# Homes of two experts in float32 at a time, and 18 load slots, in a two-layer trunk with a routed feed-forward

## The chip, the cores and the metric

The kernel runs on one core of a Trainium2 chip. The metric is the device time of one execution, in microseconds (us), as the median of three runs.

## The reference, cut to what matters

Two layers act on `x` (256 tokens of 1024 numbers, float32). Each has a mixing part (attention, pooling, memory attention, gates) and a feed-forward part. That of layer 0 is dense; that of layer 1 sends each token to two of eight experts:

```
logits = ht @ w_router
vals, idx = lax.top_k(logits, TOP_K)
gates = jax.nn.softmax(vals, axis=-1)
comb = einsum('tk,tke->te', gates, one_hot(idx, N_EXPERTS))
for e in range(N_EXPERTS):
    out = out + comb[:, e:e + 1] * ((silu(ht @ w1[e]) * (ht @ w3[e])) @ w2[e])
```

Here `ht` is the RMS-normalised `x`, with gain `norm_ffn`. The weights of one expert are three matrices of 1024 x 3584 float32.

## The kernel before, in words

All weights stream through one class, `Stream` (lines 154 to 242), in an order that `plan` (line 48) writes out. A load is 1 MB (128 partitions of 2048 float32) and holds two units. SP issues the loads in that order, and each goes into a slot, which is a tile of the name given to `widen` (line 180). `load` (line 194) issues a load for every slot in the deque `free`; `give` (line 224) puts a slot back after its second unit has been used, and calls `load`. `widen(tags, uses)` limits how often a slot serves, and `retire` (line 186) takes a slot out: at once if it is free, else after the load that it holds.

Up to the end of layer 1's mixing part every weight is split by ACT and DVE into a high and a low float32r part (`split`, line 207) and PE multiplies three combinations (line 391). The experts' weights are used as float32 straight from the slot. The eight places of experts are filled with the routed experts so that place p has `ROWS[p]` rows: 96, 64, 96, 96, 64, 96, 96, 64. "Expert" means such a place below. Layer 1 then goes like this:

- The router: `logits` while the last tall product runs, then the top two, `pos`, `place` (the slot of a token in its expert, lines 979 to 993) and the reciprocal norm `rx[3]`.
- Lines 997 to 999: `x` times `rx[3]` is split into two float32r tiles `xs` in the homes B0 and B1.
- `prep_g` (line 1002) makes G, a 0/1 matrix of tokens by rows, in the home `bb`, for a list of experts. `prep_t` (line 1012) has PE transpose it and ACT copy it into GT (home E5), which holds all experts. `gather` (line 1022) multiplies `xs` by G (line 1040) to bring the rows of the experts into XG, with the gain put on by ACT and DVE in turn (lines 1044, 1046).
- Expert 0 is gathered at once, into E2. Experts 1 to 4 are gathered together (320 columns) into E6 and E7, and 5 to 7 (256 columns) into E2; which, when and where stands in `GROUPS` (line 1222).
- `half_all` (line 1132) computes half of expert 0's first 512 inner columns for all tokens, from `h2T` (homes E6, E7), and `sel_T` picks its rows with `G[0]`.
- `STEPS` is the list of 8 experts x 7 chunks of 512 inner columns. In turn i the loop at line 1223 runs `up(i)` (line 1157: four loads, w1 and w3) and `down(i - 1)` (line 1190: two loads, w2). Both work on 32 x 32 pieces of PE: line 1172 into `acc`, line 1198 into `y`. For each unit `pump` (line 354) takes one piece of side work from the deques `fa` and `fb`.
- After an expert's last chunk `down` copies `y` to `yf` in pieces of 32 x 256, odd j by DVE (line 1212) and even j by ACT (line 1214). A bank of `y` holds two groups of 32 rows (`y[r // 2]`). `evac_split` (line 363; here lines 365, 366) makes a high and a low part, and `scatter` (line 1118) multiplies GT by both and adds the weighted result to `total` (line 1126).
- After the loop `finish` (line 841) writes the result.

The slots, by name: raw0 to raw3 from the start; E0, E1, E3, E2 (one use) and bias from line 900; E4, E5, A1, A0 from line 954, in the middle of the last tall products; pair0 to pair3 from line 1227, after `half_all`, where A1 and E5 are retired because `total` and GT need them. E2 serves once, as XG needs it.

Of the kernel before, what the change touches and what calls it, by code (L numbers as in the profile page):

```python
# [10 lines left out]
F32 = mybir.dt.float32  # L11
# [7 lines left out]
D = 1024  # L19
# [226 lines left out]
def trunk(ctx: ExitStack, tc: tile.TileContext, a, out, stage=99):  # L246
# [651 lines left out]
    parts = mix(1, hold["hT"], rx[2], hold["mT"], rm)  # L898

    W.widen(("E0", "E1", "E3"))  # L900
    W.widen(("E2",), 1)
    W.widen(("bias",))
    misc = own("band", [128, 1088], name="misc")
    used = [0]

# [47 lines left out]

    ss = branch_end(1, *parts, ready_moe, lambda: W.widen(("E4", "E5", "A1", "A0")))
    drain()
    if stage == 2:
        finish((nc.gpsimd, nc.gpsimd))
        return
# [35 lines left out]
    count = ms([128, NE])  # L994
    nc.vector.tensor_copy(count, pos[:, 2])
    rstd_of(rx[3], ss)
    xs = [own(t, [128, 2, D], F32R, name="xs") for t in ("B0", "B1")]
    for tb in range(2):
        evac_split(x[:, tb], xs[0][:, tb], xs[1][:, tb], rx[3][:, tb:tb + 1])
    G, XG, GT = {}, {}, []  # L1000

    def prep_g(es):

        at = np.cumsum([0] + [ROWS[e] for e in es])
        g = own("bb", [128, 2, at[-1]], F32R, name="G")
        for j, e in enumerate(es):
            G[e] = g[:, :, at[j]:at[j + 1]]
            for tb in range(2):
                nc.vector.tensor_scalar(G[e][:, tb], slot[:, :ROWS[e]], place[:, tb, e:e + 1], None, op0=OP.is_equal)
        G[tuple(es)] = g  # L1010

    def prep_t(e):

        if not GT:
            GT.append(own("E5", [max(ROWS), NE, 2, 128], F32R, name="GT"))
        t = mbank("gTp", (128, 2, 128))
        n = ROWS[e]
        for tb in range(2):
            nc.tensor.transpose(t[:n, tb], G[e][:, tb].bitcast(F32), ident)
        nc.scalar.activation(GT[0][:n, e], t[:n], AF.Copy)  # L1020

    def gather(es, homes):


        at = np.cumsum([0] + [ROWS[e] for e in es])
        n = at[-1]
        per = 1 if n > 256 else 2 if n > 128 else 4
        each = 8 // len(homes)

        def part(k0):  # L1030
            if k0 == 0:
                tiles = [own(t, [128, each, n], name="xg") for t in homes]
                for j, e in enumerate(es):
                    XG[e] = lambda k, j=j: tiles[k // each][:, k % each, at[j]:at[j + 1]]
                XG[tuple(es)] = lambda k: tiles[k // each][:, k % each]
            t = mbank("xgp", (128, per, n))
            for i in range(per):
                ps = [(p[:, tb, (k0 + i) * 128:(k0 + i + 1) * 128], G[tuple(es)][:, tb]) for p in xs for tb in range(2)]
                for m, (s, g) in enumerate(ps):
                    nc.tensor.matmul(t[:, i], s, g, start=m == 0, stop=m == len(ps) - 1)  # L1040
            for i in range(per):
                k = k0 + i
                if k % 2:
                    nc.vector.tensor_scalar(XG[tuple(es)](k), t[:, i], col("norm_ffn", 1, k), None, op0=OP.mult)
                else:
                    nc.scalar.activation(XG[tuple(es)](k), t[:, i], AF.Copy, scale=col("norm_ffn", 1, k))

        return [lambda k0=k0: part(k0) for k0 in range(0, 8, per)]

    prep_g([0])  # L1050
    for f in gather([0], ["E2"]):
        f()
    oh = ms([128, 2, 2, NE])
    vm, gates = ms([128, 2, 2]), ms([128, 2, 2])
# [62 lines left out]

    def scatter(e, ys, tb, j):
        t = mbank("sc")
        for p in range(2):  # L1120
            nc.tensor.matmul(t, GT[0][:ROWS[e], e, tb], ys[p][:, j * 512:(j + 1) * 512], start=p == 0, stop=p == 1)  # L1121
        if not total:
            total.append(own("A1", [128, 2, D], name="total"))
        sl = slice(j * 512, (j + 1) * 512)
        xo = total[0][:, tb, sl]
        nc.vector.scalar_tensor_tensor(xo, t, comb[:, tb, e:e + 1], x[:, tb, sl] if e == 0 else xo,  # L1126
                                       op0=OP.mult, op1=OP.add)
# [4 lines left out]
    def half_all():  # L1132


        accs = [acc_tile() for _ in range(2)]
        gs = []

        def ep():
            for tb in range(2):
                g = junk()[:, :256]  # L1140
                nc.scalar.activation(g, accs[tb][0][:, :256], AF.Silu, scale=rx[3][:, tb:tb + 1])
                nc.vector.scalar_tensor_tensor(g, accs[tb][1][:, :256], rx[3][:, tb:tb + 1], g, op0=OP.mult, op1=OP.mult)
                gs.append(g)

        def sel_T():
            t = mbank("ge0", (128, 2, ROWS[0]))
            for q in range(2):
                for tb in range(2):
                    nc.tensor.matmul(t[:, q], gs[tb][:, q * 128:(q + 1) * 128], G[0][:, tb].bitcast(F32),
                                     start=tb == 0, stop=tb == 1)  # L1150
            for q in range(2):
                nc.scalar.activation(gts[0][:, :, q], t[:, q].rearrange("p (r t) -> p r t", r=3), AF.Copy)

        run(pairs_of(256), st_of(h2T), lambda tb, b: accs[tb][b], 2, ep)
        fa.append(sel_T)

    def up(i, e, width):
# [7 lines left out]
        for k0 in range(0, 8, count):  # L1165
            w, home = W.raw()
            for m in range(count):
                k = k0 + m
                for r in range(nr):
                    t, c0 = acc[r // per], r % per * n  # L1170
                    for j in TILES:
                        nc.tensor.matmul(t[32 * j:32 * j + 32, c0:c0 + n], XG[e](k)[:, 32 * r:32 * r + 32],  # L1172
                                         w[:, (4 * m + j) * n:(4 * m + j + 1) * n],
                                         start=k == 0 and r % per == 0, stop=k == 7, tile_position=(0, 32 * j), skip_group_check=True)
            W.give(home)
            if k0 + count < 8:
                pump()
# [12 lines left out]
    def down(i, e, first, last):  # L1190
        gt = gts.pop(i)
        n = ROWS[e]
        for q in range(4):
            w, home = W.raw()
            for r in range(n // 32):
                t, c0 = y[r // 2], r % 2 * 256
                for j in TILES:
                    nc.tensor.matmul(t[32 * j:32 * j + 32, c0:c0 + 256], gt[:, r, q], w[:, 256 * j:256 * j + 256],  # L1198
                                     start=first and q == 0 and r % 2 == 0, stop=last and q == 3,
                                     tile_position=(0, 32 * j), skip_group_check=True)  # L1200
            W.give(home)
            if q < 3:
                pump()
        if last:
            yf = work.tile([n, D], F32, tag="S4", name="yf", bufs=3)
            yh, yl = (work.tile([n, D], F32R, tag="S4", name="ys", bufs=3) for _ in range(2))
            for r in range(n // 32):
                for j in TILES:
                    o = yf[32 * r:32 * r + 32, 256 * j:256 * j + 256]
                    v = y[r // 2][32 * j:32 * j + 32, r % 2 * 256:r % 2 * 256 + 256]  # L1210
                    if j % 2:
                        nc.vector.tensor_copy(o, v)  # L1212
                    else:
                        nc.scalar.activation(o, v, AF.Copy)  # L1214
            evac_split(yf, yh, yl)
            fb.extend([lambda: None] * 2)
            for b in range(2):
                for tb in range(2):
                    fb.append(lambda tb=tb, b=b: scatter(e, (yh, yl), tb, b))
        pump()  # L1220

    GROUPS = {0: ([1, 2, 3, 4], ["E6", "E7"]), 4: ([5, 6, 7], ["E2"])}
    for i in range(len(STEPS) + 1):
        if i == 0:
            new_gt(0)
            half_all()
            W.widen([f"pair{j}" for j in range(PAIRB)])
            W.retire(("A1", "E5"))
            W.load()
            places()  # L1230
            up(0, 0, 64)
        elif i < len(STEPS):
            e, c = STEPS[i]
            if e in GROUPS and c == 3:
                es, homes = GROUPS[e]
                if e == 0:
                    fb.append(lambda: prep_t(0))
                fb.append(lambda es=es: prep_g(es))
                fb.extend([lambda e_=e_: prep_t(e_) for e_ in es])
                fb.extend(gather(es, homes))  # L1240
            new_gt(i)
            up(i, e, 128)
        if i >= 1:
# [1 line left out]
            if i == 1:  # L1245
                drain()
            if c2 == 0:
                y = [pm.tile([128, 512], F32, tag=f"y{b}", name=f"y{b}", bufs=1) for b in range(-(-ROWS[e2] // 64))]
            down(i - 1, e2, c2 == 0, c2 == FE // 512 - 1)
    drain()  # L1250
    where = plan()[1]
# [117 lines left out]
```

## Time and profile before

| | us |
|---|---|
| median of three runs | 1659.22 |
| lowest, highest | 1658.77, 1660.36 |
| the profiled execution | 1658.55 |
| its span, first to last instruction | 1656.8 |
| PE busy in the span | 1615.1 |
| DVE busy | 651.0 |
| ACT busy | 529.7 |

One execution was traced. PE is TensorE's matrix products, PEld its weight loads, DVE is VectorE, ACT ScalarE, SP the engine that issues the loads. Times of the trace count from the start of the span. Each matrix product of float32 operands shows as two PE instructions, one of float32r operands as one. Busy PE is not PE at its peak: ends of products are modelled. The granted clock of PE is given as a share of its full 2.4 GHz; the other level is 1.2 GHz. A line of the chain is start, duration and what was on it; "x24" is a count of instructions, and some per cent of PE's records are missing.

### The profile page before, as it was taken

The numbers are of one execution on the slowest core, as the hardware profiler recorded it, in microseconds if no ns is written. First come the engines' busy times: TensorE is split into PE (matmuls) and PEld (weight loads), VectorE is DVE, ScalarE is ACT, GpSimd is POOL, SyncE is SP. The second block draws the span as 40 slices with busy tenths as digits, with TensorE's granted clock in tenths as the row PEclk, the third lists the DMA queues.
The fourth block names the chain that finished last, engine by engine and source line by source line (L and its number), as shares of the span: only waits on it lengthen the run. The fifth ranks groups of instructions, "written<-read, shape, count | busy, mean of one in ns | idle before, by whom it ended". The sixth has DMA issues, their size and how long they took to land.

```text
span 1656.8 us, 40623 instructions
## 1 busy us (share of the span) xinstructions
PE 1615.1 (97%) x18103; PEld 1119.8 (68%) x18103; DVE 651.0 (39%) x1270; ACT 529.7 (32%) x898; POOL 8.4 (1%) x37
## 2 busy tenths in 40 slices
PE   9999999999999999999999999999999999999986
PEld 6887778788888887788756555665655556556543
DVE  6676876555555767776310202002011020110201
ACT  6675755544554666645210100001010010100100
POOL 0000000000000000000000000000000000000000
PEclk9999999999999999999999999999999999999998
DMA  9534455444554434666779999999999999999994
GB/s 376 202 148 155 148 206 184 178 178 178 181 194 172 174 137 165 232 231 235 300 285 390 414 418 418 417 417 419 418 418 413 418 418 417 417 418 407 416 414 195
DMA packets 69606, 493.86 MB, mean 298 GB/s; under 512 B 7888, under 2 KB 7888, under 8 KB 10544
## 3 DMA queue, kind: packets, MB, share of 16 engines
q1 hardware_dynamic: 67680, 485.55, 74.1%
q0 software_dynamic: 1312, 5.08, 1.0%
q8 instruction: 144, 2.36, 0.6%
q10 hardware_dynamic: 432, 0.56, 0.1%
q14 instruction: 38, 0.31, 0.1%
HBM read 490.11 MB, written 1.05 MB: 296 GB/s over the span
## 4 chain that ended last, share of the span: by engine, by line
PE 83%; DMA 13%; DVE 2%; ACT 1%; issue 0%; SPq 0%; ACTq 0%; DVEq 0%; POOLq 0%
PE acc L391 41%; PE acc L1172 22%; DMA raw<-in_w_dram 13%; PE y L1198 12%; PE sc L1121 1%; PE ds L641 1%; DVE yf L1212 1%; PE xgp L1040 1%; PE tT L503 1%; PE do L677 1%; PE dt L666 1%; ACT yf L1214 0%; ACT ys L365 0%; PE mo L586 0%; PE ms L553 0%
## 5 line engine op out<-in xcount | busy, mean ns | idle before, releaser
L1172 PE MATMUL acc<-raw,xg 128*32 128x256 f32 (+1 forms) x9408 | 533.6, 378 | 11.4 <-DMA raw<-in_w_dram 10.8
L1172 PEld LDWEIGHTS acc<-raw,xg 128*32 128x32 f32 x9408 | 305.2, 110 | 220.5 <-issue 18.8
L219 DVE TENSOR_TENSOR pair<-raw,pair 128x1024 fp32r<-128x1024 f32 (+1 forms) x247 | 300.4, 1219 | 212.3 <-ACT pair L218 211.8
L391 PE MATMUL acc<-pair,bigB 128*128 128x512 f32 x1536 | 378.4, 401 | 1.8 <-DVE pair L219 1.7
L218 ACT ACTIVATE pair<-raw 128x1024 fp32r<-128x1024 f32 (+1 forms) x247 | 260.2, 1056 | 304.5 <-PE acc L391 289.5
L391 PEld LDWEIGHTS acc<-pair,bigB 128*128 128x128 f32 x1536 | 284.9, 189 | 67.7 <-DVE pair L219 2.1
L1183 DVE TENSOR_TENSOR junk<-acc,junk 128x256 f32<-128x256 f32 (+2 forms) x90 | 30.4, 369 | 624.0 <-ACT junk L1182 624.0
L1198 PE MATMUL y<-raw,gt 128*32 128x256 f32 x4704 | 269.0, 379 | 6.7 <-DMA raw<-in_w_dram 6.6
L1182 ACT ACTIVATE junk<-acc 128x256 f32<-128x256 f32 (+2 forms) x90 | 30.8, 343 | 681.9 <-PE acc L1172 680.3
L1198 PEld LDWEIGHTS y<-raw,gt 128*32 128x32 f32 x4704 | 153.8, 110 | 110.1 <-issue 7.8
L391 PE MATMUL acc<-pair,bigA 128*128 128x512 f32 (+1 forms) x960 | 219.9, 386 | 0.7 <-ACT g L814 0.3
L391 PEld LDWEIGHTS acc<-pair,bigA 128*128 128x128 f32 x960 | 172.3, 188 | 39.1 <-ACT g L814 0.8
L391 PE MATMUL acc<-pair,E 128*128 128x512 f32 x456 | 109.1, 396 | 0.9 <-DVE E L738 0.9
L391 PEld LDWEIGHTS acc<-pair,E 128*128 128x128 f32 x456 | 84.6, 188 | 20.3 <-DVE E L738 1.8
L1121 PE MATMUL sc<-ys,GT 96*128 96x512 f32 (+1 forms) x64 | 27.6, 506 | 12.4 <-ACT ys L365 12.0
L1185 DVE STREAM_TRANSPOSE gt<-junk 128x128 f32<-128x128 f32 (+1 forms) x147 | 34.5, 282 | 0.8
L1212 DVE COPY yf<-y 32x256 f32<-32x256 f32 x42 | 17.7, 422 | 41.0 <-ACT yf L1214 40.4
L1121 PEld LDWEIGHTS sc<-ys,GT 96*128 96x128 f32 (+1 forms) x64 | 11.4, 211 | 29.7 <-ACT ys L365 15.8
L1126 DVE SCALAR_TENSOR_TENSOR total<-sc,misc,total 128x512 f32<-128x512 f32 x28 | 20.6, 749 | 26.0 <-PE sc L1121 25.9
L1214 ACT ACTIVATE yf<-y 32x256 f32<-32x256 f32 x42 | 15.7, 374 | 47.0 <-PE y L1198 38.6
L646 DVE CUSTOM_DVE_ANT_0 dp<-ds,bias 128x128 f32<-128x128 f32 (+1 forms) x64 | 20.8, 353 | 21.6 <-PE ds L641 21.5
L650 ACT ACTIVATE dp<-dp,dmn 128x128 f32<-128x128 f32 (+1 forms) x64 | 28.5, 446 | 1.8 <-DVE dmn L646 1.2
(243 smaller groups left out, 780.0 us busy)
## 6 DMA issues: line engine op xcount, KB each, us to landing
raw<-in_w_dram SPq DMA_DIRECT2D x455, 1024.0 KB, 20.0
bb<-in_b_gate_dram POOLq DMA_DIRECT2D x6, 512.0 KB, 4.3
E<-in_mem_t_dram SPq DMA_DIRECT2D x2, 1024.0 KB, 11.4
raw<-in_w_dram SPq DMA_DIRECT2D x4, 256.0 KB, 10.5
raw<-in_w_dram SPq DMA_DIRECT2D x2, 512.0 KB, 13.0
x<-in_x_dram SPq DMA_DIRECT2D x1, 1024.0 KB, 14.1
E<-in_mem_dram SPq DMA_DIRECT2D x1, 1024.0 KB, 19.9
bias<-in_bias_dram POOLq DMA_DIRECT2D x1, 1024.0 KB, 7.5
```

The costliest lines, as they stand in the source:

```text
L218: nc.scalar.activation(t[:, 0, sl], src[:, sl], AF.Copy)
L219: nc.vector.tensor_tensor(t[:, 1, sl], src[:, sl], t[:, 0, sl].bitcast(F32), OP.subtract)
L391: nc.tensor.matmul(accs(tb, b)[:, :n], s, w[:, off:off + n], start=begin and (tb, b) not in started, stop=end and n_ == 2 and last[b] == ( ...
L646: nc.vector.tensor_tensor_reduce(p[:, 0, m, :kl], t[m][:, :kl], bias[:, h, 256 - kl:], 1.0, 3e38, OP.add, OP.min, mn[:, m:m + 1])
L650: nc.scalar.activation(p[:, 1, m, :kl], p[:, 0, m, :kl], AF.Exp, scale=-1.0, bias=mn[:, m:m + 1], accum_out=s0[:, b, h:h + 1] if m == 0 el ...
L1121: nc.tensor.matmul(t, GT[0][:ROWS[e], e, tb], ys[p][:, j * 512:(j + 1) * 512], start=p == 0, stop=p == 1)
L1172: nc.tensor.matmul(t[32 * j:32 * j + 32, c0:c0 + n], XG[e](k)[:, 32 * r:32 * r + 32], w[:, (4 * m + j) * n:(4 * m + j + 1) * n], start=k = ...
L1182: nc.scalar.activation(g[:, r0:r1], v[:, :, 0], AF.Silu)
L1183: nc.vector.tensor_tensor(g[:, r0:r1], v[:, :, 1], g[:, r0:r1], OP.mult)
L1185: nc.vector.transpose(gts[i][:, r, 4 - width // 32:].rearrange("p q t -> p (q t)"), g[:, r])
L1198: nc.tensor.matmul(t[32 * j:32 * j + 32, c0:c0 + 256], gt[:, r, q], w[:, 256 * j:256 * j + 256], start=first and q == 0 and r % 2 == 0, st ...
L1212: nc.vector.tensor_copy(o, v)
```

## The change

- `xs` and its split go. G is made with `rx[3]` as its value in place of 1, and the gather multiplies `x` itself by G, both float32, two products for each block in place of four.
- Expert 0's XG and G sit in a tile of the tag S4; a second tile there, `here`, holds a 0/1 matrix for `sel_T`. The others are gathered for two experts at a time, [1, 2], [3, 4], [5, 6], [7], in turns of chunk 3 of experts 0, 2, 4, 6, in E6 and E7 by turns, with G in the same tile.
- GT holds two experts, in `bb`. `prep_t` runs once in each expert, and DVE makes GT as 1 where the transposed G is above 0.
- One bank of the gathered rows is evacuated by ACT, the next by DVE.
- E2 and E5 stay slots, B0 and B1 become slots after the last tall product, E7 serves as a slot twice after `half_all`. Only A1 is retired.
- `y` always has two banks; row group r lies in bank r % 2, and is copied by DVE for odd r, by ACT for even r.
- The last expert's rows are scattered as float32 without the split.

```diff
-    W.widen(("E2",), 1)
-    W.widen(("bias",))
+    W.widen(("E2", "bias"))
...
     drain()
+    W.widen(("B0", "B1"))
...
-    xs = [own(t, [128, 2, D], F32R, name="xs") for t in ("B0", "B1")]
-    for tb in range(2):
-        evac_split(x[:, tb], xs[0][:, tb], xs[1][:, tb], rx[3][:, tb:tb + 1])
-    G, XG, GT = {}, {}, []
+    G, XG, GT, flags = {}, {}, {}, {}
+    back = own("bb", [max(ROWS), 2, 2, 128], F32R, name="GT")
...
+        n = at[-1]
+        home = tile_([128, 10 * n])
+        XG[tuple(es)] = home[:, :8 * n].rearrange("p (k a) -> p k a", k=8)
+        g = home[:, 8 * n:].rearrange("p (t a) -> p t a", t=2)
...
+                nc.vector.tensor_scalar(G[e][:, tb], slot[:, :ROWS[e]], place[:, tb, e:e + 1], rx[3][:, tb:tb + 1],
+                                        op0=OP.is_equal, op1=OP.mult)
...
-            nc.tensor.transpose(t[:n, tb], G[e][:, tb].bitcast(F32), ident)
-        nc.scalar.activation(GT[0][:n, e], t[:n], AF.Copy)
+            nc.tensor.transpose(t[:n, tb], G[e][:, tb], ident)
+        GT[e] = back[:n, e % 2]
+        nc.vector.tensor_scalar(GT[e], t[:n], 0.0, None, op0=OP.is_gt)
...
+        per = 2 if n > 128 else 4
...
+                for tb in range(2):
+                    nc.tensor.matmul(t[:, i], x[:, tb, (k0 + i) * 128:(k0 + i + 1) * 128], G[tuple(es)][:, tb],
+                                     start=tb == 0, stop=tb == 1)
...
+                if k0 // per % 2:
+                    nc.vector.tensor_scalar(XG[tuple(es)][:, k], t[:, i], col("norm_ffn", 1, k), None, op0=OP.mult)
...
-    prep_g([0])
-    for f in gather([0], ["E2"]):
+    prep_g([0], lambda shape: s4(shape, "xg"))
+    here = s4([128, 2, ROWS[0]], "here")
+    for tb in range(2):
+        nc.vector.tensor_scalar(here[:, tb], slot, place[:, tb, 0:1], None, op0=OP.is_equal)
+    for f in gather([0]):
...
+        gt = GT[e] if len(ys) == 2 else GT[e].bitcast(F32)
+        for p in range(len(ys)):
+            nc.tensor.matmul(t, gt[:, tb], ys[p][:, j * 512:(j + 1) * 512], start=p == 0, stop=p == len(ys) - 1)
...
-                t, c0 = y[r // 2], r % 2 * 256
+                t, c0 = y[r % 2], r // 2 * 256
...
+            for j in TILES:
+                for r in range(n // 32):
                     o = yf[32 * r:32 * r + 32, 256 * j:256 * j + 256]
+                    v = y[r % 2][32 * j:32 * j + 32, r // 2 * 256:r // 2 * 256 + 256]
+                    if r % 2:
                         nc.vector.tensor_copy(o, v)
                     else:
                         nc.scalar.activation(o, v, AF.Copy)
+            ys = (yf,)
+            if e < NE - 1:
+                ys = tuple(work.tile([n, D], F32R, tag="S4", name="ys", bufs=3) for _ in range(2))
+                evac_split(yf, *ys)
+                fb.extend([lambda: None] * 2)
...
-    GROUPS = {0: ([1, 2, 3, 4], ["E6", "E7"]), 4: ([5, 6, 7], ["E2"])}
+    GROUPS = {0: ([1, 2], "E6"), 2: ([3, 4], "E7"), 4: ([5, 6], "E6"), 6: ([7], "E7")}
...
-            W.retire(("A1", "E5"))
+            W.retire(("A1",))
+            W.widen(("E7",), 2)
...
+            if c == 3:
+                fb.append(lambda e_=e: prep_t(e_))
...
-                y = [pm.tile([128, 512], F32, tag=f"y{b}", name=f"y{b}", bufs=1) for b in range(-(-ROWS[e2] // 64))]
+                y = [pm.tile([128, 512], F32, tag=f"y{b}", name=f"y{b}", bufs=1) for b in range(2)]
```

## Rows read from the trace of the kernel before

**Rows 1.** The page's slices, 40 of 41.4 us: PE busy, load rate.

```profile
PE   9999999999999999999999999999999999999986
...
GB/s 376 202 148 155 148 206 184 178 178 178 181 194 172 174 137 165 232 231 235 300 285 390 414 418 418 417 417 419 418 418 413 418 418 417 417 418 407 416 414 195
```

**Rows 2.** Stretches: us, busy PE, PEld, DVE, ACT, POOL, clock, DMA share, GB/s.

```profile
780.00:802.00 22.00, 21.98 (x165) 20.63 (x164) 16.36 (x66) 12.71 (x23) 0.00 (x0) 0.92 0.52 192
...
805.00:925.00 120.00, 120.00 (x2142) 71.96 (x2146) 13.81 (x56) 9.51 (x27) 0.00 (x0) 1.00 0.90 346
925.00:1010.00 85.00, 81.14 (x1430) 48.18 (x1426) 13.88 (x36) 6.59 (x16) 0.00 (x0) 1.00 1.01 418
...
1540.00:1637.00 97.00, 85.66 (x1452) 47.00 (x1444) 13.18 (x32) 5.98 (x14) 0.00 (x0) 1.00 0.95 390
1637.00:1657.00 20.00, 8.21 (x76) 4.54 (x72) 5.81 (x9) 2.55 (x5) 0.00 (x0) 0.70 0.21 75
```

**Rows 3.** SP's waits, 805 to 925 us: total, times, longest.

```profile
SPq L201 <- PE acc L1172: 61.0, 27, 4.5
SPq L201 <- PE y L1198: 30.7, 13, 4.0
```

**Rows 4.** SP's waits, 925 to 1640 us.

```profile
SPq L201 <- DMA raw<-in_w_dram: 497.3, 252, 3.0
```

**Rows 5.** Loads issued from 805 to 860 us, then 925 to 1010: us to landing.

```profile
raw<-in_w_dram SPq DMA_DIRECT2D x17, 1024.0 KB, 6.0
...
raw<-in_w_dram SPq DMA_DIRECT2D x38, 1024.0 KB, 19.9
```

**Rows 6.** The chain from 1630 us to the end: start, us, what.

```profile
1617.35 20.19 DMA raw<-in_w_dram
...
1637.67 3.69 PE y L1198 x64
...
1641.45 0.38 ACT yf L1214
...
1641.86 0.42 DVE yf L1212
...
1644.89 1.06 ACT ys L365
...
1646.00 1.22 PE sc L1121 x2
...
1651.00 0.75 DVE total L1126
```

**Rows 7.** The chain from 1105 to 1165 us: expert 2 to 3, 96 rows.

```profile
1117.71 4.79 PE y L1198 x88
...
1138.57 5.18 PE y L1198 x96
1143.75 10.36 PE acc L1172 x192
```

**Rows 8.** PE's timeline in expert 4, 64 rows: one `up`.

```profile
1290.51 7.09 PE L1172 MATMUL acc<-raw,xg 128*32 128x256 f32 x128
```

**Rows 9.** The chain: a transpose and one part of each later gather.

```profile
850.55 0.34 PE gTp L1019 x2
...
852.32 0.79 PE xgp L1040 x4
...
1253.48 1.37 PE xgp L1040 x10
```

**Rows 10.** PE's timeline: four float32 instructions of layer 0; expert 0's gather.

```profile
58.00 1.03 PE L542 MATMUL py<-pds,pw 128*128 128x256 f32 x4
...
795.10 4.12 PE L1040 MATMUL xgp<-G,xs 128*128 128x96 f32 x32
```

**Rows 11.** Groups by shape: busy us, mean ns of one.

```profile
L542 PE MATMUL py<-pds,pw 128*128 128x256 f32 x16 | 4.1, 380 | 0.0
```

**Rows 12.** DVE's timeline in the router: the second split of `x`.

```profile
791.18 1.29 DVE L369 SCALAR_TENSOR_TENSOR xs<-x,rx,xs 128x1024 fp32r<-128x1024 f32 x1
```

More of the change, by code (lines that the diff above doesn't have):

```diff
@@ L996, in trunk, with prep_g @@
     rstd_of(rx[3], ss)
-    xs = [own(t, [128, 2, D], F32R, name="xs") for t in ("B0", "B1")]
-    for tb in range(2):
-        evac_split(x[:, tb], xs[0][:, tb], xs[1][:, tb], rx[3][:, tb:tb + 1])
-    G, XG, GT = {}, {}, []
-    def prep_g(es):
+    G, XG, GT, flags = {}, {}, {}, {}
+    back = own("bb", [max(ROWS), 2, 2, 128], F32R, name="GT")
+    def prep_g(es, tile_):
         at = np.cumsum([0] + [ROWS[e] for e in es])
-        g = own("bb", [128, 2, at[-1]], F32R, name="G")
+        n = at[-1]
+        home = tile_([128, 10 * n])
+        XG[tuple(es)] = home[:, :8 * n].rearrange("p (k a) -> p k a", k=8)
+        g = home[:, 8 * n:].rearrange("p (t a) -> p t a", t=2)
@@ L1006, in prep_g @@
         for j, e in enumerate(es):
+            XG[e] = XG[tuple(es)][:, :, at[j]:at[j + 1]]
             G[e] = g[:, :, at[j]:at[j + 1]]
             for tb in range(2):
-                nc.vector.tensor_scalar(G[e][:, tb], slot[:, :ROWS[e]], place[:, tb, e:e + 1], None, op0=OP.is_equal)
+                nc.vector.tensor_scalar(G[e][:, tb], slot[:, :ROWS[e]], place[:, tb, e:e + 1], rx[3][:, tb:tb + 1],
+                                        op0=OP.is_equal, op1=OP.mult)
         G[tuple(es)] = g
@@ L1012, in prep_t @@
     def prep_t(e):
-        if not GT:
-            GT.append(own("E5", [max(ROWS), NE, 2, 128], F32R, name="GT"))
+        n = ROWS[e]
         t = mbank("gTp", (128, 2, 128))
-        n = ROWS[e]
         for tb in range(2):
-            nc.tensor.transpose(t[:n, tb], G[e][:, tb].bitcast(F32), ident)
-        nc.scalar.activation(GT[0][:n, e], t[:n], AF.Copy)
[L1022 to L1028, printed above, removed]
-        def part(k0):
[L1031 to L1035, printed above, removed]
+            nc.tensor.transpose(t[:n, tb], G[e][:, tb], ident)
@@ L1036, in part, with gather @@
+        GT[e] = back[:n, e % 2]
+        nc.vector.tensor_scalar(GT[e], t[:n], 0.0, None, op0=OP.is_gt)
+    def gather(es):
+        n = sum(ROWS[e] for e in es)
+        per = 2 if n > 128 else 4
+        def part(k0):
             t = mbank("xgp", (128, per, n))
             for i in range(per):
-                ps = [(p[:, tb, (k0 + i) * 128:(k0 + i + 1) * 128], G[tuple(es)][:, tb]) for p in xs for tb in range(2)]
-                for m, (s, g) in enumerate(ps):
-                    nc.tensor.matmul(t[:, i], s, g, start=m == 0, stop=m == len(ps) - 1)
+                for tb in range(2):
+                    nc.tensor.matmul(t[:, i], x[:, tb, (k0 + i) * 128:(k0 + i + 1) * 128], G[tuple(es)][:, tb],
+                                     start=tb == 0, stop=tb == 1)
@@ L1041, in part @@
             for i in range(per):
                 k = k0 + i
-                if k % 2:
-                    nc.vector.tensor_scalar(XG[tuple(es)](k), t[:, i], col("norm_ffn", 1, k), None, op0=OP.mult)
+                if k0 // per % 2:
+                    nc.vector.tensor_scalar(XG[tuple(es)][:, k], t[:, i], col("norm_ffn", 1, k), None, op0=OP.mult)
                 else:
-                    nc.scalar.activation(XG[tuple(es)](k), t[:, i], AF.Copy, scale=col("norm_ffn", 1, k))
+                    nc.scalar.activation(XG[tuple(es)][:, k], t[:, i], AF.Copy, scale=col("norm_ffn", 1, k))
@@ L1119, in scatter @@
         t = mbank("sc")
-        for p in range(2):
-            nc.tensor.matmul(t, GT[0][:ROWS[e], e, tb], ys[p][:, j * 512:(j + 1) * 512], start=p == 0, stop=p == 1)
+        gt = GT[e] if len(ys) == 2 else GT[e].bitcast(F32)
+        for p in range(len(ys)):
+            nc.tensor.matmul(t, gt[:, tb], ys[p][:, j * 512:(j + 1) * 512], start=p == 0, stop=p == len(ys) - 1)
         if not total:
@@ L1148, in sel_T @@
                 for tb in range(2):
-                    nc.tensor.matmul(t[:, q], gs[tb][:, q * 128:(q + 1) * 128], G[0][:, tb].bitcast(F32),
+                    nc.tensor.matmul(t[:, q], gs[tb][:, q * 128:(q + 1) * 128], here[:, tb],
                                      start=tb == 0, stop=tb == 1)
@@ L1171, in up @@
                     for j in TILES:
-                        nc.tensor.matmul(t[32 * j:32 * j + 32, c0:c0 + n], XG[e](k)[:, 32 * r:32 * r + 32],
+                        nc.tensor.matmul(t[32 * j:32 * j + 32, c0:c0 + n], XG[e][:, k, 32 * r:32 * r + 32],
                                          w[:, (4 * m + j) * n:(4 * m + j + 1) * n],
@@ L1195, in down @@
             for r in range(n // 32):
-                t, c0 = y[r // 2], r % 2 * 256
+                t, c0 = y[r % 2], r // 2 * 256
                 for j in TILES:
                     nc.tensor.matmul(t[32 * j:32 * j + 32, c0:c0 + 256], gt[:, r, q], w[:, 256 * j:256 * j + 256],
-                                     start=first and q == 0 and r % 2 == 0, stop=last and q == 3,
+                                     start=first and q == 0 and r < 2, stop=last and q == 3,
                                      tile_position=(0, 32 * j), skip_group_check=True)
@@ L1205, in down @@
             yf = work.tile([n, D], F32, tag="S4", name="yf", bufs=3)
-            yh, yl = (work.tile([n, D], F32R, tag="S4", name="ys", bufs=3) for _ in range(2))
-            for r in range(n // 32):
-                for j in TILES:
+            for j in TILES:
+                for r in range(n // 32):
                     o = yf[32 * r:32 * r + 32, 256 * j:256 * j + 256]
-                    v = y[r // 2][32 * j:32 * j + 32, r % 2 * 256:r % 2 * 256 + 256]
-                    if j % 2:
+                    v = y[r % 2][32 * j:32 * j + 32, r // 2 * 256:r // 2 * 256 + 256]
+                    if r % 2:
                         nc.vector.tensor_copy(o, v)
@@ L1214, in down @@
                         nc.scalar.activation(o, v, AF.Copy)
-            evac_split(yf, yh, yl)
-            fb.extend([lambda: None] * 2)
+            ys = (yf,)
[3 more added lines that the diff above has]
+                fb.extend([lambda: None] * 2)
             for b in range(2):
                 for tb in range(2):
-                    fb.append(lambda tb=tb, b=b: scatter(e, (yh, yl), tb, b))
+                    fb.append(lambda tb=tb, b=b: scatter(e, ys, tb, b))
         pump()
-    GROUPS = {0: ([1, 2, 3, 4], ["E6", "E7"]), 4: ([5, 6, 7], ["E2"])}
+    GROUPS = {0: ([1, 2], "E6"), 2: ([3, 4], "E7"), 4: ([5, 6], "E6"), 6: ([7], "E7")}
     for i in range(len(STEPS) + 1):
@@ L1233, in trunk @@
             e, c = STEPS[i]
+            if c == 3:
+                fb.append(lambda e_=e: prep_t(e_))
             if e in GROUPS and c == 3:
[L1235 to L1240, printed above, removed]
+                es, home = GROUPS[e]
+                fb.append(lambda es=es, home=home: prep_g(es, lambda shape: own(home, shape, name="xg")))
+                fb.extend(gather(es))
             new_gt(i)
```

## Prediction

> **What bounds the kernel now.** First the slices of the page [rows 1]: after its first slice the load rate lies between 137 and 300 GB/s over the first half, climbs, and is flat near 417 until the last slice, while PE shows 9 almost everywhere. Two resources look full, so the slices alone do not say which sets the end. Next the table by stretch [rows 2]: from 805 to 925 us PE is busy in all of its 120 us and the DMA engines move 346 GB/s; from 925 to 1010 us they move 418 GB/s at a share of 1.01 and PE loses 3.9 of 85 us. Then the waits of SP's own queue. Up to 925 us SP waits for PE to free a slot, 40 times in the two rows shown, 91.7 us together [rows 3]; after that it waits 252 times, 497.3 us, for an earlier load to land [rows 4], and a load takes 19.9 us from issue to landing where it took 6.0 [rows 5]. So the number of slots paces the loads until about 925 us and the transfer rate paces them afterwards. The chain agrees at its end: the last weight load is on it up to 1637.5 us [rows 6].
>
> From the switch on, the end is the bytes still missing over the rate. One load is 1,048,576 bytes, at 418 GB/s 2.51 us. A step is six loads, 15.05 us. PE needs 10.36 + 5.18 = 15.54 us for a step of 96 rows [rows 7]; a step of 64 rows has two thirds of the instructions, 6.91 + 3.45 = 10.36 us (the row of 128 instructions shows 7.09 with its own latency, [rows 8]). So an expert of 64 rows (1, 4 and 7) uses up 7 x 4.69 = 32.8 us of lead, 13.1 loads, which the others build up slowly.
>
> **The change, part by part.** *Slots.* Before, 14 slots stay in the rotation while the experts run: raw0-3, E0, E1, E3, bias, E4, A0, pair0-3 (E2 serves once; A1 and E5 are retired). After it E2, E5, B0 and B1 stay too: 18. E7 also serves twice; at some 16 loads of distance and 2.6 us of PE per load both uses are over at about 802 + 2 x 45 = 890 us, so I give it nothing. As long as slots pace the loads, four more of them mean four more loads fetched at the switch: 4 x 2.51 = **10.0 us less**. There is room: 418 less 346 GB/s over 120 us is 8.6 MB, and four loads are 4.2 MB. Ends: 0 if they are not filled in time, 15 if E7's two loads still count at the switch.
>
> *PE before the switch.* Here slots are freed by PE, so PE time moves the loads with it. The gather for experts 1 to 4 was 8 blocks of 0.79 us, 6.3 us, and five transposes of G at 0.34 us [rows 9]. Now there are two experts of 160 columns in float32, and each product is two instructions. The nearest float32 rows: four instructions of 256 columns in 1.03 us, of 0.38 us each [rows 10, 11], so one follows another after (1.03 - 0.38) / 3 = 0.217 us, 0.85 ns a column. 160 columns: 0.136 us, 32 instructions 4.3 us, and some 0.2 us of changeover for each of four parts, 5.1 us. Gain 1.2, and four transposes fewer, 1.4: **2.6 us less**. Ends: 0 (the price of 256 columns for each, 6.9 us, and parts that wait for their copies) to 4. Expert 0's gather stays at 32 instructions with weights of the same size, 4.1 us before [rows 10]: nothing, up to 1 us either way.
>
> *Router stretch.* The split of x into xs goes, two instructions of ACT and two of DVE of 1.29 us [rows 12], and two small comparisons for `here` come. PE is busy 21.98 of 22 us there [rows 2] with half_all's matmuls, which hide it: nothing. If that cover went, DVE's path to G would be shorter by 1.3 us or longer by 0.5. B0 and B1 sit in SP's queue ahead of later loads, but their last reader is over at about 782 us, so nothing queues behind them; E7 waits for the same matmuls as pair0-3.
>
> *PE after the switch.* Three more gathers: 5.1 us, 32 x 0.163 + 0.8 = 6.0 us for 192 columns, 4.1 us for 64, and seven transposes of 0.35: 17.7 us. Before: 4 parts, 4.6 us together (a row of ten instructions is 1.37 us), and three transposes, 5.7 us [rows 9]. So **12 us more of PE, costed at nothing** because the loads pace this stretch; what that cover is worth is the first rival. Moving the copy of GT from ACT to DVE, and each bank's evacuation to one engine, goes with it: both engines are nearly idle there.
>
> *Tail.* From PE's last product to the last sum: 1641.4 to 1651.75 us, 10.3 us [rows 6]. The eight copies of yf take turns, ACT at 1641.45, DVE at 1641.86 and so on until 1644.87, 3.4 us, and all of them read one bank. On two banks, four copies of 0.43 us run on each side, 1.7 us; if something other than the bank makes them take turns, this term is nothing. The ACT split of 1.06 us goes. A scatter of 512 columns in float32 is 2 x 512 x 0.85 ns = 0.87 us; four of them, 0.3 us of latency and a last sum of 0.75 make 4.5 us, against 5.75 now (1646.00 to 1651.75). Sum 1.7 + 1.06 + 1.25: **4.0 us less**. Ends: 5 less if the first scatter starts on half of the copies, 1 more if copies still alternate and the scatters run at the lower clock (granted 0.70 in the last 20 us, [rows 2]; four scatters would be 3.5 us longer). The Trainium skill, PSUM — Partial Sum Buffer, section "PSUM bank collisions raise a hardware error", says that two engines may use one bank at the same time where they touch different groups of 32 partitions. These copies do, so by that rule they could run side by side already and the second bank would bring nothing: 14.9 us in all instead of 16.6. [rows 6] shows that in this program they wait for each other all the same, so I keep the 1.7.
>
> **Sum:** 10.0 + 2.6 + 4.0 = 16.6 us. Against the profiled execution, 1658.55 us for a span of 1656.8, that is 1641.95; the median of the runs, 1659.22, lies 0.67 higher, so I predict **1642.6 us**. A measurement of this kernel can tell about 0.2%, 3.3 us, from no change.
>
> **Rivals.** *A. PE takes over.* What PE alone needs from 924.5 us: 28 full steps of 96 rows, 435.1; 20 products up and 21 down of 64 rows, 210.6; seven changes of expert, each 5.3 us over its product (from 1117.71 + 5.18 to 1138.57, less 10.36, [rows 7]); the gather, 5.7: it would be through at 1613, where it is through at 1641.4. The forecast brings the loads to 1628.8 and PE to 1613 - 2.6 + 12 = 1622. Under seven us of margin is thin on prices this rough. If the parts cost half as much again, 9 us, PE is through near 1631 to 1634, and the time is 1645 to 1648. *B. The lead is not kept.* The four slots fill but the switch comes earlier because loads and slots run nearly even (15.05 against 15.54 us a step): only the PE term and the tail count, 1652.6. Against it: the 8.6 MB of room and 91.7 us of waiting for slots. *C. Slower.* PE falls to the lower of its two clocks while it waits for loads. A 64-row step at 1.2 GHz takes 20.7 us against 15.05 of loads; an expert so spent costs 7 x 5.7 = 40 us, and some 23 us net, 1682; it decides from about three steps on. The rows speak against it: granted 1.00 in both stretches where PE waits for loads [rows 2]. The Trainium skill, TensorE: Matmul & The Clock Gate, section "HAM oscillation — how this bites in real kernels", tells of loops whose work per tile is shorter than the wait for its transfer and which fall back to the lower clock each time; this trace has such waits without the fall, so C keeps a small chance. *D. The change does not do what it says:* loads go out only some eight at a time (19.9 us over 2.51, [rows 4, 5]), so slots beyond that could be idle; then only the tail would count, 1655. But 40 waits for slots deny it.
>
> **How the numbers follow.** Forecast 0.66, A 0.20, B 0.07, C 0.04, D 0.03. The forecast's own range is 1636.5 (E7's loads, or the early scatter and the router) to 1646; A reaches 1648. To leave out no more than 2 in 10, with the bounds above: 1636 to 1649. Faster by over 0.2%: all but C, and 0.02 of B and D, whose times come close to the bound: 0.94; within: 0.02; slower: 0.04.
>
> **What would show it.** Right: SP's waits change from PE to loads near 922 us, with 4 loads more landed than before by then; expert 1 ends some 7 us earlier; 416 to 418 GB/s until the end; last load near 1625 us; tail of about 6 us with copies side by side. Wrong: PE without idle in experts 4 to 7 (A); 418 GB/s well ahead of 900 us (B); a granted clock under 0.95 in a stretch of tens of us (C); SP waiting for loads where it now waits for PE (D).

## The result and the profile after

The changed kernel takes 1642.57 us in the median (four runs, 1641.30 to 1643.18) against 1659.22 (1658.77 to 1660.36): a ratio of 0.9898, 95% interval 0.9881 to 0.9915. That is 16.65 us less; 16.6 were forecast. (Measured again, experiment 9, it took 1641.55 beside 1660.31, 18.8 us less.) The profiled execution took 1641.3 us for a span of 1640.0.

The page's slices, 40 of 41.0 us, answer to [rows 1]: PE busy and the load rate.

```profile
PE   9999999999999999999999999999999999999998
...
GB/s 376 205 145 163 141 198 189 175 181 179 189 192 162 186 139 159 203 247 280 334 335 392 395 418 417 418 417 418 417 418 404 418 417 417 418 418 417 412 406 228
```

The slices from the 18th to the 21st carry more than before, and the last is fuller; the plateau is the same. By stretch (columns as in [rows 2]: us, busy PE, PEld, DVE, ACT, POOL, clock, DMA share, GB/s):

```profile
780.00:805.00 25.00, 24.84 (x278) 22.87 (x280) 17.92 (x83) 11.40 (x24) 0.00 (x0) 1.00 0.86 336
...
805.00:925.00 120.00, 117.73 (x2132) 71.25 (x2124) 13.62 (x50) 10.07 (x27) 0.00 (x0) 1.00 0.95 370
925.00:1010.00 85.00, 84.53 (x1469) 49.11 (x1470) 15.67 (x36) 5.53 (x14) 0.00 (x0) 1.00 1.01 410
```

One row of the kernel before that was not shown, for its first stretch:

```profile
780.00:805.00 25.00, 24.67 (x227) 22.63 (x225) 19.01 (x79) 14.57 (x25) 0.00 (x0) 0.93 0.51 186
```

From 780 to 925 us the changed kernel loads 336 x 25 + 370 x 120 = 52.8 MB where the one before loaded 186 x 25 + 346 x 120 = 46.2 MB [rows 2]. The 6.6 MB are 6.3 loads. PE is 4.1 us further by then and has used 1.6 of them (2.6 us a load), so the lead at the switch is larger by about 4.7 loads. The four slots are filled, and most of it happens between 780 and 805 us. In these 25 us SP had stood 13.6 us at one slot; it now stands there 1.9 us (before, then after):

```profile
SPq L201 <- DVE rx L459: 13.6, 1, 13.6
```

```profile
SPq L201 <- DVE rx L472: 1.9, 1, 1.9
```

With 14 slots this wait is 13.6 us again, with 16 it is 5.6 (experiments 1 and 2). That fits more free slots standing ahead of the held one in the queue, which no run tests by itself.

SP's waits in the changed kernel, 805 to 925 us and then 925 to 1640 us (total, times, longest), answer to [rows 3, 4]:

```profile
SPq L201 <- PE acc L1171: 69.8, 29, 5.0
SPq L201 <- PE y L1197: 29.2, 14, 2.2
...
SPq L201 <- DMA raw<-in_w_dram: 365.0, 202, 3.0
SPq L201 <- PE acc L1171: 112.7, 81, 3.8
SPq L201 <- PE y L1197: 54.5, 41, 2.8
```

The switch is still there, but after it SP waits 167 us for PE to free a slot, where before this was some 49 us:

```profile
SPq L201 <- PE acc L1172: 33.2, 45, 4.9
SPq L201 <- PE y L1198: 15.6, 14, 2.7
```

What PE waited for between 925 us and its last product tells the other half. First before, then after:

```profile
PE acc L1172 <- DMA raw<-in_w_dram: 10.8, 18, 1.0
PE sc L1121 <- ACT ys L365: 7.3, 7, 1.8
PE y L1198 <- DMA raw<-in_w_dram: 6.6, 12, 0.8
```

```profile
PE sc L1120 <- ACT ys L365: 9.6, 7, 2.2
...
PE y L1197 <- DMA raw<-in_w_dram: 0.2, 1, 0.2
```

PE's waits for loads went from 17.4 us to 0.2. The loads no longer set the pace alone: PE keeps step with them nearly everywhere. The page puts 93% of the chain on PE (83% before):

```profile
PE 93%; DMA 4%; ACT 2%; DVE 1%; issue 0%; ACTq 0%; SPq 0%; DVEq 0%; POOLq 0%
```

The end of the chain answers to [rows 6] (start, us, what):

```profile
1603.61 19.82 DMA raw<-in_w_dram
...
1623.57 3.69 PE y L1197 x64
...
1628.28 1.95 PE sc L1120 x4
...
1630.31 3.30 PE sc L1120 x4
...
1633.63 0.75 DVE total L1125
```

The last load lands at 1623.43 us in place of 1637.54, 14.1 us earlier. From the last product's end (1627.26) to the last sum's end (1634.38) there are 7.1 us in place of 10.4. What follows the last sum is 0.6 us longer. 14.1 + 3.3 - 0.6 is the change of the span, 16.8 us.

### The profile page after: what moved, and what is told of

Its sections match the earlier page's. It is cut to its first block, busy times and chain, and to the rows that moved or that the text cites. A ratio compares the mean times of both kernels' runs of the same rounds, so it can differ in the third digit from the quotient of the medians.

```text
span 1640.0 us, 40766 instructions
## 1 busy us (share of the span) xinstructions
PE 1615.9 (99%) x18167; PEld 1123.9 (69%) x18167; DVE 649.1 (40%) x1275; ACT 527.0 (32%) x904; POOL 8.4 (1%) x37
## 4 chain that ended last, share of the span: by engine, by line
PE 93%; DMA 4%; ACT 2%; DVE 1%; issue 0%; ACTq 0%; SPq 0%; DVEq 0%; POOLq 0%
PE acc L391 41%; PE acc L1171 28%; PE y L1197 14%; DMA raw<-in_w_dram 3%; PE sc L1120 2%; PE xgp L1034 1%; PE ds L641 1%; ACT yf L1212 1%; PE tT L503 1%; PE do L677 1%; PE dt L666 1%; ACT ys L365 0%; PE mo L586 0%; PE ms L553 0%; DMA bb<-in_lam_dram 0%
## 5 line engine op out<-in xcount | busy, mean ns | idle before, releaser
L1171 PEld LDWEIGHTS acc<-raw,xg 128*32 128x32 f32 x9408 | 301.5, 110 | 206.9 <-issue 15.5
L1120 PE MATMUL sc<-ys,GT 96*128 96x512 f32 (+1 forms) x56 | 22.7, 479 | 10.3 <-ACT ys L365 9.6
L1212 ACT ACTIVATE yf<-y 32x256 f32<-32x256 f32 x52 | 19.5, 375 | 37.1 <-PE y L1197 36.6
L1034 PEld LDWEIGHTS xgp<-xg,x 128*128 128x128 f32 x160 | 21.3, 190 | 6.3 <-issue 6.2
```

Of the source, the lines that this page charges most:

```text
L1034: nc.tensor.matmul(t[:, i], x[:, tb, (k0 + i) * 128:(k0 + i + 1) * 128], G[tuple(es)][:, tb], start=tb == 0, stop=tb == 1)
L1120: nc.tensor.matmul(t, gt[:, tb], ys[p][:, j * 512:(j + 1) * 512], start=p == 0, stop=p == len(ys) - 1)
L1171: nc.tensor.matmul(t[32 * j:32 * j + 32, c0:c0 + n], XG[e][:, k, 32 * r:32 * r + 32], w[:, (4 * m + j) * n:(4 * m + j + 1) * n], start=k = ...
```

## The experiments

Two theories were set against each other: L, the loads pace the experts after the switch and PE is hidden; P, PE paces the changed kernel throughout, as its missing waits suggest (rival A of the prediction). Each kernel is the changed one with the edit shown. Where parts of a time are compared, they are those of the profiled executions, one of each kernel.

**1. 14 slots (slots14).** The four homes leave the rotation as before.

```diff
-    W.widen(("E2", "bias"))
+    W.widen(("E2",), 1)
+    W.widen(("bias",))
...
-    W.widen(("B0", "B1"))
...
-            W.retire(("A1",))
+            W.retire(("A1", "E5"))
```

> The changed kernel with 14 slots in the rotation: B0 and B1 are not slots, E2 serves once, E5 is retired; everything else as changed. Theory L (loads pace the experts after the switch, each of the four slots is worth one load of 2.51 us): lead when expert 1 starts about 10.5 to 11 loads instead of 15.1, last load and end 10.0 us later, 1652.6 us. Theory P (PE paces the changed kernel throughout, as no 64-row expert shows a wait for loads any more): the first part of the lost lead costs nothing, so 3 to 7 us, 1646 to 1650. Theory N (the slots bring nothing, the gain is PE's): 1642.6.

1651.33 us (0.9945 of before, interval 0.9931 to 0.9959), 8.8 us above the changed kernel: between P's 1650 and L's 1652.6. PE's waits for loads are back (925 to 1640 us):

```profile
PE acc L1171 <- DMA raw<-in_w_dram: 5.5, 11, 0.7
PE y L1197 <- DMA raw<-in_w_dram: 5.2, 8, 1.4
```

The last load lands at 1635.17 us, 11.7 later than in the changed kernel:

```profile
1614.46 20.71 DMA raw<-in_w_dram
```

In time the slots are worth 8.8 us of the 10.0 forecast. By the last load they are worth more; part of that is hidden, because this kernel's tail took 5.8 us at a granted 1.00 where the changed kernel's took 7.1 (experiment 8). The rest of the change, with 14 slots, is also 7.9 to 8.8 us better than before (1659.22 on the first chip, 1660.14 beside this run); forecast for PE's part and the tail were 6.6. In the profiled executions it is 6.5 us of the span: 2.4 at the last load and 4.6 in the tail, less 0.5 behind it.

**2. 16 slots (slots16).** Only `W.widen(("B0", "B1"))` is left out.

> The changed kernel with 16 slots: only B0 and B1 are left out. Theory L: two loads, 5.0 us, 1647.6 us, lead at expert 1 about 13. Theory P: under 2.5 us, 1643 to 1645, since PE's own work would still hide most of it. Theory N: 1642.6.

1644.88 us, 2.3 us above the changed kernel. By the time alone that is P's reading for the last two slots: 6.5 us for the first two, 2.3 for the last two. The profile says otherwise:

```profile
1608.47 19.77 DMA raw<-in_w_dram
...
1628.38 3.69 PE y L1196 x64
...
1635.11 1.97 PE sc L1119 x4
```

The last load lands at 1628.24 us, 4.8 later than in the changed kernel, where L has 5.0. The difference shrinks behind it: the second pair of scatters takes 1.97 us at a granted 1.00, where the changed kernel's took 3.30 at the lower clock, and what follows the last sum is 0.7 us shorter. By the last load the first two slots are worth 6.9 us and the last two 4.8, against 5.0 forecast for each pair.

**3. Later gathers left out (no_gather).** Places 3 to 7 use the rows and G of place 1 or 2 of the same size, so the gathers for [3, 4], [5, 6] and [7] and their G are left out; loads and the experts' products are as many as before.

```diff
                 es, home = GROUPS[e]
-                fb.append(lambda es=es, home=home: prep_g(es, lambda shape: own(home, shape, name="xg")))
-                fb.extend(gather(es))
+                if e == 0:
+                    fb.append(lambda es=es, home=home: prep_g(es, lambda shape: own(home, shape, name="xg")))
+                    fb.extend(gather(es))
+                else:
+                    for e_ in es:
+                        G[e_], XG[e_] = (t[1 if ROWS[e_] == 64 else 2] for t in (G, XG))
```

> The changed kernel without the three later gathers (places 3 to 7 use the rows and G of places 1 and 2 of the same size; 17 us of PE's work after the switch left out). Theory L: the same time, at most 2 us less, with new PE waits for loads in experts 4 and 7. Theory P: the end moves with PE, 8 us or more less, 1635 or below, until the loads bind. If the two limits have met: 1 to 3 us less.

1640.67 us (1639.27 to 1643.40), 1.9 us less in the median, with runs that overlap the changed kernel's (1641.30 to 1643.18). Some 15 us of work went and less than 2 came back. These waits (925 to 1640 us) are those of the slowest of the four runs, whose last load landed at 1625.73 us:

```profile
PE acc L1171 <- DMA raw<-in_w_dram: 8.3, 12, 2.1
PE y L1197 <- DMA raw<-in_w_dram: 5.9, 9, 1.6
```

So the loads stand right behind PE. P, which had 8 us or more less, falls as the only cause of the time, although PE has 93% of the chain on the changed kernel's page; L holds within about 2 us.

**4. Both edits (slots14_no_gather).**

> Both edits together: 14 slots, and the three later gathers left out. Theory L: as slots14 alone, 1652.6 us, since PE's work is hidden behind the loads. Theory P: less than slots14 by what slots14 lost, near the time of no_gather plus a few us.

1650.78 us, 0.5 us from experiment 1. With 14 slots the loads pace alone, and the gathers are fully hidden, as L has it:

```profile
PE acc L1171 <- DMA raw<-in_w_dram: 11.5, 20, 0.7
PE y L1197 <- DMA raw<-in_w_dram: 9.6, 15, 2.2
```

**5. The last split put back (last_split).** `if e < NE - 1:` becomes `if True:`, so the last expert is split and scattered in two halves.

> The changed kernel, but the last expert's rows are split into a high and a low part again before its scatter. Read from the last product's end to the last sum, 7.1 us in the changed kernel's profile. Forecast: 1.06 us for ACT's split and 1.25 us for the scatters come back, 9.4 us, time 2.3 us longer, 1644.9. Rival (a float32 scatter costs as much as both halves, so only the split's own time counts): 1 us or less.

1645.51 us (1643.04 to 1645.82), 2.9 us more, with 2.3 forecast. But only part of it is the split. In its profile the tail has 8.7 us from the last product (1629.59) to the last sum (1638.28), 1.6 more than the changed kernel's: between the forecast and its rival. The last product itself ends 2.3 us later, by parts that the edit does not touch: expert 1 starts at 909.89 us in place of 908.69, and a spell at the lower clock more stands from 1120 to 1140 us (granted 0.91, where the changed kernel has 1.00). The scatters' share of the 1.6 depends on the clock, which is told under experiment 8.

**6. One bank (one_bank).** The old mapping of `y`, both in the products (with the start flag that goes with it) and in the copies.

```diff
-                t, c0 = y[r % 2], r // 2 * 256
+                t, c0 = y[r // 2], r % 2 * 256
...
-                    v = y[r % 2][32 * j:32 * j + 32, r // 2 * 256:r // 2 * 256 + 256]
+                    v = y[r // 2][32 * j:32 * j + 32, r % 2 * 256:r % 2 * 256 + 256]
```

> The changed kernel with the old mapping of y (two row groups per bank) and copies by ACT and DVE in turn by row group. Forecast: the last expert's eight copies take turns again, 3.4 us where the changed kernel's profile has 1.7, so the tail is 1.7 us longer, 1644.3. Rival (the two engines may use one bank at once where they touch different partitions): the copies stay side by side, 1642.6.

1646.92 us (1643.95 to 1648.46), 4.3 us more. The chain of its tail shows the copies in turn again:

```profile
1629.82 0.38 ACT yf L1212
...
1630.22 0.42 DVE yf L1210
...
1630.67 0.38 ACT yf L1212
...
1631.07 0.43 DVE yf L1210
...
1631.55 6.63 PE sc L1120 x8
```

The first scatter starts 1.8 us after the last product, where it started after 1.0 us in the changed kernel, and then its eight instructions take 6.63 us in place of 5.3: the granted clock was 0.57 from 1631 to 1639 us. So the tail is 2.1 us longer, 0.8 of it by the copies, where 1.7 were forecast; the last product ends 2.5 us later. The copies' own order is shown; how much of the 4.3 us is theirs is not, since they also stand at every change of expert. The Trainium skill's rule that the two engines may work on different groups of 32 partitions of one bank (PSUM — Partial Sum Buffer, section "PSUM bank collisions raise a hardware error") is neither confirmed nor denied here. In this kernel the ACT copy and the DVE copy after it read the same 32 partitions; in the kernel before they read different ones and took turns all the same [rows 6]. In both the engines wait for each other's semaphores, so the bank's own limit never comes up.

**7. Later scatters (later_scatter).** `fb.extend([lambda: None] * 2)` becomes `* 4`.

> The changed kernel with two more turns of side work between an expert's copies and its scatters (four empty turns in place of two), so that PE does not wait for the split rows: some 1.3 us of idle PE in each of seven experts, 9 us. Theory L: nothing, PE is hidden behind the loads, 1642.6. Theory P: up to 9 us less, 1634. If the two limits have met: 1 to 2 us less, as no_gather.

1640.10 us (1639.67 to 1640.69), 2.5 us less. PE's wait for ACT's split fell from 9.6 to 3.0 us, and waits for loads took their place:

```profile
PE acc L1171 <- DMA raw<-in_w_dram: 3.8, 7, 0.7
PE sc L1120 <- ACT ys L365: 3.0, 4, 0.9
PE y L1197 <- DMA raw<-in_w_dram: 2.9, 5, 0.7
```

Another way to lighten PE, and again some 2 us: the last load landed at 1622.13 us, and the loads were in the way.

**8. E7 not a slot (no_e7).** `W.widen(("E7",), 2)` is left out.

> The changed kernel without E7's two uses as a slot. Forecast: both are over before the switch, so nothing: 1642.6, lead at expert 1 about 15. Rival: its loads still count at the switch: up to 2.5 us for each still held, 1645 to 1647.

1639.15 us (1638.77 to 1639.70), 3.4 us *less*. Neither side had that. The profiled executions differ by 2.5 us: 0.5 at the last product, 1.3 in the tail, 0.7 behind the last sum. Two differences stand in them. The changed kernel's PE has a pause before the second `up`, which the profile puts down to nothing that it shows (timeline of PE, 807 to 811 us):

```profile
809.08 2.15 PE L1171 MATMUL acc<-raw,xg 128*32 128x256 f32 x36 [1.05 <-issue]
```

No row with a pause stands there in no_e7. The nine profiles with E7 as a slot all have one, of 0.71 to 1.11 us, and start expert 1 at 908.4 to 910.1 us; the three without (with the two below) start it at 907.2 to 907.4. And at the end, the second pair of scatters takes 1.97 us where it took 3.30 (chain of no_e7's tail):

```profile
1602.49 20.46 DMA raw<-in_w_dram
...
1623.09 3.69 PE y L1197 x64
...
1627.79 1.95 PE sc L1120 x4
...
1629.82 1.97 PE sc L1120 x4
...
1631.81 0.75 DVE total L1125
```

Over these last stretches the granted clock was 1.00 in no_e7 and 0.86 in the changed kernel:

```profile
1623.00:1632.00 9.00, 7.57 (x72) 3.76 (x72) 4.12 (x8) 1.50 (x4) 0.00 (x0) 1.00 0.19 71
```

```profile
1623.50:1633.70 10.20, 8.89 (x72) 4.02 (x72) 4.00 (x8) 1.50 (x4) 0.00 (x0) 0.86 0.19 69
```

This second difference is not E7's by itself: the kernels of experiments 1 and 2 use E7 as a slot and have the full clock there.

**9 to 11. The changed kernel and no_e7 once more, and no_e7 with later scatters**, side by side on one chip.

> The changed kernel itself, beside the next two on one chip. If the 3.4 us between it and no_e7 come from E7's use or from what it does to the order of instructions, it is again near 1642.6; if they were a difference between chips or hours, it is near no_e7.

> no_e7 once more: near 1639.2 if the gain repeats, with no PE pause of 1 us near 808 us and the last scatters at the full clock; near 1642.6 if it does not.

> no_e7 and later_scatter together. Theory that loads and PE have met: no_e7 leaves PE 1.3 us ahead, later_scatter takes PE's idle time at the changes of expert away, and the loads set the end: the last load lands near 1622 us as in both alone, so 1637 to 1639, not the sum of the two gains (1636.7 or less). Theory P: 9 us below no_e7, 1630.

1641.55 us (1641.02 to 1642.87), 1639.77 (1638.70 to 1639.96) and 1640.05 (1638.94 to 1640.70). Side by side the runs of no_e7 and of the changed kernel do not overlap, so the gain repeats, at 1.8 us here and 3.4 against the first measurement. The pause stands in the changed kernel's second profile (1.01 us) and in neither of the two without E7; why E7's loads bring it is not settled. The two gains do not add: no_e7_later is where no_e7 and later_scatter are alone, 1 us above the 1637 to 1639 expected, and its last load lands at 1623.0 us. In the four lightened kernels whose last load is on the chain (no_gather, later_scatter, no_e7, no_e7_later) it lands between 1622.1 and 1625.7 us, however much of PE's work or waiting is gone: about where the loads alone set the end. The best version is the changed kernel without E7 as a slot: 0.9874 of the kernel before (interval 0.9858 to 0.9891).

## Why the prediction was right, step by step

- **Slots, 10.0 us forecast.** Experiment 1 measured 8.8 in time and 11.7 at the last load. The mechanism was as forecast: slots pace the loads up to the switch, the lead there grew by 4.7 loads, expert 1's last product ended 6.6 us earlier (some 7 forecast), and the last load landed 14.1 us earlier (12.6 forecast for the slots and PE together). One transfer for each slot held about: 6.9 us at the last load for the first two, 4.8 for the last two, where 5.0 was the price of each pair.
- **PE before the switch, 2.6 us forecast.** With 14 slots, so without the slots' share, the last load lands at 1635.17 in place of 1637.54 us: 2.4. PE itself is 4.1 us ahead at the switch: expert 1's first products start at 908.69 us in place of 912.79 (chain, below). A part of the new gather took 1.28 us, four make the 5.1 us of the forecast. Some of the rest is the router stretch, where 0 was forecast and PE's granted clock was 1.00 in place of 0.92 [rows 2]: the spell at the lower clock that the kernel before had there did not come. The sum also counted the changeover between main and side work for the new parts alone. 24 products between two parts take 1.43 us, an eighth of the 10.36 us of [rows 7] is 1.30, and eight such interruptions went (13 before, five after), an estimate of 1.1 us.

```profile
912.79 6.91 PE acc L1172 x128
```

```profile
908.69 6.91 PE acc L1171 x128
```

```profile
844.73 1.28 PE xgp L1034 x8
846.01 1.43 PE acc L1171 x24
...
1247.90 1.50 PE xgp L1034 x8
...
1478.85 1.93 PE xgp L1034 x16
```

- **PE after the switch, 12 us costed at nothing.** The prices held (four parts of 1.28 and of 1.50, two of 1.93 us for 64 columns: 5.1, 6.0 and 3.9 us). Costing them at nothing held to within some 2 us, by experiments 3, 4 and 7, but the margin of 6.8 us behind it was not there: PE was through at 1627.3 us, with almost no wait for loads, where 1622 was forecast for PE alone. That sum was short by 5 us. Two spells at the lower clock explain part of it, an estimate of 1.7 us each; the sum had taken all rows at full clock. PE also waited more at the changes of expert, 9.6 us for ACT's split in place of 7.3.

```profile
1230.00:1250.00 20.00, 17.80 (x212) 9.21 (x208) 7.16 (x13) 5.17 (x12) 0.00 (x0) 0.91 1.01 417
1550.00:1570.00 20.00, 17.80 (x242) 8.92 (x238) 7.16 (x13) 4.43 (x10) 0.00 (x0) 0.91 1.00 398
```

- **Tail, 4.0 us forecast, 3.3 measured.** The copies run side by side and the first scatter starts after half of them, the end named as 5 us; then the clock fell within the scatters and gave 1.3 us back. At the full clock (experiment 8) the tail is 5.8 us, 4.6 less than before. Experiments 5 and 6 show the direction of the split's and the bank's share; they do not give each a clean price.
- **Rivals.** A came true in its sign (PE without waits in experts 4 to 7) and not in its price: PE arrived together with the loads, not after them. B falls by experiment 1. C did not happen; the low spells in the experts were 3.4 us each. What the prediction calls such waits, for C, were not those of the loops it cites: no wait for a load was longer than 1.0 us in the kernel before, beside steps of 10.36 to 15.54 us of work. D falls by experiments 1 and 2.
- **Luck.** In the sum, 1.5 us more than forecast at the last load, 0.7 less in the tail and 0.6 less after it met, and the second measurement of the same change had 18.8 us: the exactness of the 1642.6 is partly luck, the order of the terms is not.

## What to carry to other kernels

Where a stream of loads saturates late, a buffer more is worth about its transfer time once (2.4 to 3.5 us here, at 2.51 a transfer), at the moment when the pace passes from buffers to transfers; look for that moment in the loading queue's own waits. Work on another engine behind such a stream may be costed at nothing only after its whole remaining sum, spells at the lower clock included, has been set against the stream's end. When both meet, the chain names the engine that came last by a hair: 93% of the chain lay on PE, and taking 15 us of its work away gained some 2 us at most. Where spells of the clock can fall into the tail, compare the landing of the last load as well as the time: two slots looked worth 2.3 us by the one and 4.8 by the other.

## What was not expected of the hardware

In the rows read, the lower clock comes in spells of 3.4 or 6.8 us, at places that move when something unrelated is edited: the kernel before had 3.4 us of it from 798 us and 6.8 from 1239, the changed kernel 3.4 from 1238 and 3.4 from 1559, and at the end it fell at 1645.0 before, at 1630.8 in the changed kernel, inside its scatters, and after the last sum without E7. A spell of 3.4 us at half of the full clock costs PE some 1.7 us (an estimate, half its length). The rows show PE with waits of some two microseconds ahead of those at the changes of expert; they do not show what decides. The Trainium skill, TensorE: Matmul & The Clock Gate, section "HAM oscillation — how this bites in real kernels", tells of a fall of the clock in loops whose work per tile is shorter than the wait for its transfer. No run here shows that case: in the kernel before, waits for loads of 1.0 us at most went with a granted 1.00, and the spells in the experts stood at the changes of expert, where PE waits for ACT and DVE.

And a slot more can cost time: with E7's two uses PE pauses some 1 us, which no row explains, and expert 1 starts at least 1 us later. Without them the time was 1.8 us less, side by side on one chip; how much of that is the pause, and how much the clock in the tail, is not settled.
